# The first block's differential heads run together with the products of the other attention's queries, and both streams of heads begin at once

## The chip, the cores and the metric

One NeuronCore of a Trainium2 chip runs the whole network in one launch. The metric is the device time of one execution in microseconds (us). A core has TensorE (PE, the matrix engine, with a queue for weight loads, PEld), VectorE (DVE), ScalarE (ACT), GpSimd (POOL) and SyncE (SP, which issues most DMAs). Each engine works through a queue of its own in order and waits at semaphores for the others. Matmuls write to PSUM, which has eight banks of 128 x 512 floats.

## What is computed

Two layers over 256 context tokens and 256 latent tokens of width 1024. Each layer has a token mixer of three kinds of heads behind one input projection (`w_in`) and one output projection (`w_out`), and then a channel mixer: a SwiGLU block in the first layer, eight experts of which each token uses two in the second. All modulation (scales, shifts, gates) comes from products of a conditioning vector with `ada_w`. The two attentions, which matter here:

```
swa : 8 window heads of 64   softmax(q k^T / 8, with a sink) v      band of keys plus all context
diff: 4 heads, two maps each w = softmax(q0 k0^T) - lam * softmax(q1 k1^T);  out = norm(w v)
lru : a gated linear recurrence in both directions, 256 channels
out = concat(lru, swa, diff) @ w_out
```

In layer 0 the queries of all four blocks of 128 tokens are needed (blocks 0 and 1 are context, 2 and 3 latent), in layer 1 those of the latent blocks alone.

## The kernel before

Every product is made in three matmuls of rounded parts (`mm3`, lines 105 to 109): a weight is split into a high and a low part by a cast on ScalarE and a subtraction on VectorE (L126, L127).

`mixer` is the function around the change. It makes, for one layer: the recurrence's inputs and its coroutines (`self.scans`, driven by `fill_lru`); the keys and values; the queries of the differential heads; at last, with the columns from 512 on, the queries of the window heads: for each block tb in `order` (2, 3, 0, 1 in layer 0; 2, 3 in layer 1) `token_major` makes 24 matmuls into a bank `acc`, `rope` (L530 to L532) turns the latent blocks, and `swa_q` splits the result (L131, L132), transposes it (L543) and casts it back (L545).

Then `streams` runs two streams of coroutines in rounds. Stream a holds `diff` for each block, stream b holds `swa`. A step of `diff` is one head map (a latent block; two of a context block): score matmul (L669), maximum (L595), scaling (L670), exponential (L674) and, for every second map, the combination (L680 to L682), the transposes of the weights (L581), their copy (L585) and the product with the values (L686) into the block's output bank. A step of `swa` does the same for a window head (L611 to L615, L623, L627, L634). Stream b starts when six rounds have gone by (`if j == 1 and n < 6: continue`). After every second round `fill(1)` emits one piece of other work from `self.todo`: in layer 0 the sixteen ada steps (a DMA of 1 MB into one of the two `raw` buffers at L253 and four matmuls into bank A at L255), in layer 1 eight ada steps and four small builds of columns and rows. What is left over is emitted after the streams by `fill(99)`.

After the streams `project` loads `w_out` through the same two `raw` buffers (L793, L796), splits it and multiplies.

PSUM banks by tag: acc 2, S 3 (scores), T 2 (transposes), A 1. The order in which the program emits an instruction is its priority; the framework that builds the program then orders each engine's queue by priority and by its own estimate of what will be ready, so that work emitted later can stand ahead of work that has to wait.

Of the kernel before, what the change touches and what calls it, by code (L numbers as in the profile page):

```python
# [24 lines left out]
P = 128  # L25
# [51 lines left out]
class Trunk:  # L77
# [246 lines left out]
            nc.vector.tensor_tensor(out=G, in0=G, in1=self.lng(*ln)[:, None, :].to_broadcast([P, 2, KD]), op=ALU.mult)  # L324
        return G, B

    def streams(self, a, b):

        rest, live, tails, n = [list(a), list(b)], [None, None], [], 0
        while any(live) or any(rest) or tails:  # L330
            tails = [g for g in tails if next(g, self) is not self]
            for j in range(2):
                if j == 1 and n < 6:
                    continue
                if live[j] is None and rest[j]:
                    live[j] = rest[j].pop(0)
                if live[j] and next(live[j]) == "tail":
                    tails.append(live[j])
                    live[j] = None
            n += 1  # L340
            if n % 2 == 0:
                self.fill(1)
# [85 lines left out]
                    part(s0, kh, cb)  # L428
                    yield bs

    def token_major(self, uh, ul, ws, tb, c1=512):

        b = self.bank("acc")
        s = slice(tb * P, (tb + 1) * P)
        for k in range(KD):
            self.mm3(b[:, 0:c1], uh[k][:, s], ul[k][:, s], ws[k][0][:, 0:c1], ws[k][1][:, 0:c1], k == 0, k == KD - 1)
        return b
# [218 lines left out]
    def diff(self, l, tb, q, kT, V, mix, mp):  # L656
# [11 lines left out]
        for h0 in range(0, 8, G):  # L668
# [7 lines left out]
            if len(Ps) == 2:  # L676
# [6 lines left out]
                t = self.weights_t(p0, nk)  # L683
# [8 lines left out]
        sq = self.rp.tile([P, 512], F32, name="ra", tag="ra")[:, 0:256]  # L692
# [19 lines left out]
        b = self.bank("T")  # L712
        for k in range(2):
            nc.tensor.transpose(b[:, k * P:(k + 1) * P], m[:, k * P:(k + 1) * P], self.eye)
        hi, lo = (t[:, :, tb * P:(tb + 1) * P] for t in mp)
        self.split2(hi, lo, b[:, 0:256].rearrange("p (k t) -> p k t", k=2))


    def mixer(self, l, uh, ul, qtb, bd, products, prepare=None):
        nc, i, tc = self.nc, self.i, self.tc  # L720
        lat = qtb[0] == 2
        order = qtb if lat else [2, 3, 0, 1]
        view = lambda c0: self.w_in(l, c0)
        t0 = 256 if lat else 0
        with tc.tile_pool(name="pp", bufs=4) as self.pp, tc.tile_pool(name="kv", bufs=1) as kp, tc.tile_pool(name="st", bufs=2) as self.sp, \
                tc.tile_pool(name="qp", bufs=len(qtb)) as self.qp, tc.tile_pool(name="rp", bufs=1) as self.rp, \
                tc.tile_pool(name="sm", bufs=2) as self.sm, ExitStack() as es:
            y = kp.tile([P, 2, T - t0], F32, name="y")
            lru = es.enter_context(ExitStack())
            self.lp = lru.enter_context(tc.tile_pool(name="lru", bufs=1))  # L730
            xs, bs = [], [*products][-1]
            for cb in range(2):
                xs.append(self.lru_in(bs[cb]))
            for cb in range(2):
                self.lru_gate(cb, bs[2 + cb], t0, y)
            self.scans = [self.lru(l, cb, xs[cb], bd, y, t0) for cb in range(2)]
            kdT = kp.tile([P, 8, T], F32R, name="kdT")
            kT = kp.tile([P, 4, T], F32R, name="kT")
            dV = kp.tile([P, NTB, 256], F32, name="dV")
            V = kp.tile([P, NTB, P], F32, name="V")  # L740
            mix = {tb: kp.tile([P, 256], F32, name=f"mix{tb}") for tb in qtb}
            ws = self.chunk(view(1536))
            for tb in range(NTB):
                b = self.token_major(uh, ul, ws, tb)
                nc.scalar.copy(out=dV[:, tb], in_=b[:, 256:512])
                src = b[:, 0:256]
                self.keys(src if tb < 2 else self.rope(src, 8, 16, tb - 2, "32"), 8, 32, kdT, tb)
                self.fill_lru(1)
            ws = self.chunk(view(1024))
            dq = {}  # L750
            for tb in range(NTB):
                b = self.token_major(uh, ul, ws, tb, 512 if tb in qtb else 256)
                nc.scalar.copy(out=V[:, tb], in_=b[:, 128:256])
                src = b[:, 0:128]
                self.keys(src if tb < 2 else self.rope(src, 2, 32, tb - 2, "64"), 2, 64, kT, tb)
                if tb in qtb:
                    src = b[:, 256:512]
                    dq[tb] = self.diff_q(src if tb < 2 else self.rope(src, 8, 16, tb - 2, "32"))
                self.fill_lru(2)
            self.fill_lru(99)  # L760
            lru.close()
            if prepare:
                prepare()
            sqp = es.enter_context(tc.tile_pool(name="sq", bufs=len(qtb)))
            ws = self.chunk(view(512))
            sq = {}
            for tb in order:
                b = self.token_major(uh, ul, ws, tb)
                sq[tb] = self.swa_q(b if tb < 2 else self.rope(b, 8, 32, tb - 2, "64"), sqp)
            (hp, mh), (lp, ml) = self.pairs("mh"), self.pairs("ml")  # L770
            c0, c1 = qtb[0] * P, (qtb[-1] + 1) * P
            for cb in range(2):
                self.split2(mh[cb][:, c0:c1], ml[cb][:, c0:c1], y[:, cb])
            self.streams([self.diff(l, tb, dq[tb], kdT, dV, mix[tb], (hp[3], lp[3])) for tb in order],
                         [self.swa(l, tb, sq[tb], kT, V, (hp[1:3], lp[1:3])) for tb in order])
            self.fill(99)
        return mh, ml

# [641 lines left out]
```

## Time and profile before

| | |
|---|---|
| median of three runs | 1669.04 us (1667.8 to 1669.34) |
| the profiled execution | 1670.24 us, its span from first to last instruction 1668.5 us |
| TensorE busy | 1584.1 us, 95% of the span |
| VectorE busy | 1217.6 us, 73% |
| ScalarE busy | 919.0 us, 55% |
| mean granted TensorE clock | 0.976 of full speed |
| products of the window queries, layer 0 / layer 1 | about 131 to 157 us / 804 to 817 us |
| the streams, layer 0 / layer 1 | about 157 to 269 us / 817 to 893 us |

A busy time is the time in which an engine had an instruction under way; ends of matmuls are modelled, since they are pipelined, so a busy TensorE need not be at its best. A granted clock of 1.00 is 2.4 GHz, 0.50 is 1.2 GHz. In timelines the columns are start, duration, engine, line, operation, the tiles written and read, the shape and the count of merged instructions, and in brackets the idle time just before and what ended it.

### The profile page before, as it was taken

The page shows a single profiled execution, that of the slowest core. Times are in us where ns is not written, and L with a number is a line of the kernel's source. Part 1 is how long each engine was busy: PE and PEld are TensorE (multiplying, and loading weights), DVE is VectorE, ACT ScalarE, POOL GpSimd, SP SyncE. Part 2 cuts the span into 40 slices and gives each one's busy share as a digit, 9 for nine tenths or more (in the row PEclk, how much of TensorE's full clock was granted, in tenths as well). Part 3 has the DMA queues.
Part 4 walks back from the last instruction along what each step waited for, and adds up shares of the span by engine and source line. Part 5 has one row for each costly group of instructions (what it writes and reads, how often), then busy time and mean ns, then how long its engine had stood idle before and what let it go on. Part 6 is the DMA issues. An engine that isn't in the chain of part 4 may idle for free. (4 is left out here: it accounts for less than half of the span.)

```text
span 1668.5 us, 21566 instructions
## 1 busy us (share of the span) xinstructions
PE 1584.1 (95%) x7977; PEld 1227.8 (74%) x7977; DVE 1217.6 (73%) x1733; ACT 919.0 (55%) x1298; POOL 161.5 (10%) x131
## 2 busy tenths in 40 slices
PE   7999999999999999999899799999999999999995
PEld 3776566787777777777567588787887878878774
DVE  2678674654543335677976898999889898888987
ACT  2466565422222223246666487777676776767773
POOL 0000012250000000350002200101001010010101
PEclk8999999999999999999999799999999999999998
DMA  8313446334443336112347599898998989989890
GB/s 310 116 54 105 152 152 202 101 114 165 159 146 125 126 126 202 51 59 78 108 146 273 181 394 357 324 377 301 352 350 320 343 310 348 355 319 331 326 359 30
DMA packets 164584, 364.79 MB, mean 219 GB/s; under 512 B 8397, under 2 KB 46121, under 8 KB 159353
## 3 DMA queue, kind: packets, MB, share of 16 engines
q1 hardware_dynamic: 159472, 355.56, 60.6%
q0 software_dynamic: 1840, 6.67, 1.2%
q10 hardware_dynamic: 3160, 1.12, 0.3%
q8 instruction: 65, 1.06, 0.3%
q14 instruction: 47, 0.38, 0.1%
HBM read 362.27 MB, written 1.05 MB: 218 GB/s over the span
## 5 line engine op out<-in xcount | busy, mean ns | idle before, releaser
L127 DVE TENSOR_TENSOR wlo<-rawb,whi 128x1024 fp32r<-128x1024 f32 x362 | 436.0, 1249 | 34.4 <-ACT whi L126 30.7
L126 ACT CAST whi<-rawb 128x1024 fp32r<-128x1024 f32 x362 | 364.4, 1052 | 55.5 <-PE ps_h L109 31.7
L127 DVE TENSOR_TENSOR wlo<-raw,whi 128x1024 fp32r<-128x1024 f32 x214 | 268.8, 1281 | 45.2 <-ACT whi L126 43.9
L126 ACT CAST whi<-raw 128x1024 fp32r<-128x1024 f32 x214 | 217.9, 1051 | 145.2 <-DMA raw<-in_ffn_w_dram 52.0
L108 PE MATMUL ps_h<-wlo,th 128*128 128x512 f32 (+1 forms) x672 | 256.6, 382 | 14.3 <-DVE wlo L127 13.4
L107 PE MATMUL ps_h<-whi,th 128*128 128x512 f32 (+1 forms) x672 | 252.8, 376 | 0.0
L109 PE MATMUL ps_h<-whi,tl 128*128 128x512 f32 (+1 forms) x672 | 250.6, 373 | 0.0
L108 PEld LDWEIGHTS ps_h<-wlo,th 128*128 128x128 f32 x672 | 126.6, 188 | 52.0 <-DVE wlo L127 31.6
L107 PEld LDWEIGHTS ps_h<-whi,th 128*128 128x128 f32 x672 | 126.6, 188 | 22.5 <-ACT th L131 0.2
L109 PEld LDWEIGHTS ps_h<-whi,tl 128*128 128x128 f32 x672 | 126.7, 188 | 20.4 <-DVE tl L132 0.2
L108 PE MATMUL ps_Y<-wlo,gTh 128*128 128x512 f32 x308 | 122.4, 397 | 0.4
L109 PE MATMUL ps_Y<-whi,gTl 128*128 128x512 f32 x308 | 120.2, 390 | 0.0
L1160 POOL TENSOR_TENSOR hl<-hl,sct 128x512 f32<-128x512 f32 x26 | 45.0, 1758 | 677.4 <-DVE sct L1159 557.3
L107 PE MATMUL ps_Y<-whi,gTh 128*128 128x512 f32 x308 | 108.4, 390 | 0.0
L890 DVE TENSOR_TENSOR silu<-silu,ps_S 128x512 f32<-128x512 f32 x22 | 15.1, 686 | 114.6 <-PE ps_S L109 114.6
L107 PE MATMUL ps_acc<-uh,whi 128*128 128x512 f32 (+1 forms) x256 | 92.1, 365 | 2.3 <-ACT whi L126 2.3
L108 PE MATMUL ps_acc<-ul,whi 128*128 128x512 f32 (+1 forms) x256 | 94.0, 367 | 0.1
L109 PE MATMUL ps_acc<-uh,wlo 128*128 128x512 f32 (+1 forms) x256 | 92.0, 360 | 0.0
L108 PE MATMUL ps_S<-ul,whi 128*128 128x512 f32 (+1 forms) x240 | 85.7, 357 | 0.0
L107 PE MATMUL ps_S<-uh,whi 128*128 128x512 f32 (+1 forms) x240 | 85.6, 357 | 0.0
L109 PE MATMUL ps_S<-uh,wlo 128*128 128x512 f32 (+1 forms) x240 | 85.0, 355 | 0.0
L107 PE MATMUL ps_acc<-whi,uh 128*128 128x512 f32 (+1 forms) x176 | 71.0, 403 | 0.0
(352 smaller groups left out, 2881.4 us busy)
## 6 DMA issues: line engine op xcount, KB each, us to landing
rawb<-in_moe_w_dram SPq DMA_DIRECT2D x181, 1024.0 KB, 7.0
raw<-in_moe_w_dram SPq DMA_DIRECT2D x50, 1024.0 KB, 6.9
raw<-in_ada_w_dram SPq DMA_DIRECT2D x40, 1024.0 KB, 4.9
raw<-in_ffn_w_dram SPq DMA_DIRECT2D x33, 1024.0 KB, 5.6
raw<-in_w_in_dram SPq DMA_DIRECT2D x16, 1024.0 KB, 5.1
aw<-in_ada_w_dram SPq DMA_DIRECT2D x16, 512.0 KB, 6.7
raw<-in_w_out_dram SPq DMA_DIRECT2D x16, 512.0 KB, 5.9
lg<-in_ln_g_dram POOLq DMA_DIRECT2D x4, 512.0 KB, 4.1
```

The source lines that it names most:

```text
L107: mm(out, lhsT=ah, rhs=bh, start=start, stop=False)
L108: mm(out, lhsT=ah, rhs=bl, start=False, stop=False)
L109: mm(out, lhsT=al, rhs=bh, start=False, stop=stop)
L126: nc.scalar.copy(out=hi, in_=v)
L127: self.last = nc.vector.tensor_tensor(out=lo, in0=v, in1=hi, op=ALU.subtract)
L890: nc.vector.tensor_tensor(out=t, in0=t, in1=b3, op=ALU.mult)
L1160: (nc.vector if quick and nn else nc.gpsimd).tensor_tensor(out=hl[:, b, cs], in0=hl[:, b, cs], in1=t, op=ALU.add)
```

## The change

`streams` takes the first coroutine of stream a as it stands (`live`) and starts stream b in the first round. `mixer` creates the differential coroutines before the products of the window queries. After the first three blocks' products in layer 0 it advances the first of them by two steps each, after each of the two blocks in layer 1 by three: six steps in either layer. The products go to banks acc and A in turn, since the first coroutine takes one of the two acc banks for its output. The output tiles of `diff` are handed over by a function, as they are allocated only after the products.

```diff
-    def streams(self, a, b):
+    def streams(self, a, b, live):
 
-        rest, live, tails, n = [list(a), list(b)], [None, None], [], 0
+        rest, live, tails, n = [list(a), list(b)], [live, None], [], 0
         while any(live) or any(rest) or tails:
             tails = [g for g in tails if next(g, self) is not self]
             for j in range(2):
-                if j == 1 and n < 6:
-                    continue
                 if live[j] is None and rest[j]:
...
-    def token_major(self, uh, ul, ws, tb, c1=512):
+    def token_major(self, uh, ul, ws, tb, c1=512, bank="acc"):
 
-        b = self.bank("acc")
+        b = self.bank(bank)
...
-        hi, lo = (t[:, :, tb * P:(tb + 1) * P] for t in mp)
+        hi, lo = (t[:, :, tb * P:(tb + 1) * P] for t in mp())
...
-            for tb in order:
-                b = self.token_major(uh, ul, ws, tb)
+            out = []
+            parts = [self.diff(l, tb, dq[tb], kdT, dV, mix[tb], lambda: out) for tb in order]
+            for j, tb in enumerate(order):
+                b = self.token_major(uh, ul, ws, tb, bank=("acc", "A")[j % 2])
                 sq[tb] = self.swa_q(b if tb < 2 else self.rope(b, 8, 32, tb - 2, "64"), sqp)
+                if j < 3:
+                    for _ in range(3 if lat else 2):
+                        next(parts[0])
             (hp, mh), (lp, ml) = self.pairs("mh"), self.pairs("ml")
+            out += [hp[3], lp[3]]
...
-            self.streams([self.diff(l, tb, dq[tb], kdT, dV, mix[tb], (hp[3], lp[3])) for tb in order],
-                         [self.swa(l, tb, sq[tb], kT, V, (hp[1:3], lp[1:3])) for tb in order])
+            self.streams(parts[1:], [self.swa(l, tb, sq[tb], kT, V, (hp[1:3], lp[1:3])) for tb in order], parts[0])
             self.fill(99)
```

## Rows read from the trace of the kernel before

**Rows 1.** The page, busy time of each engine (share of the span), instructions.

```profile
PE 1584.1 (95%) x7977; PEld 1227.8 (74%) x7977; DVE 1217.6 (73%) x1733; ACT 919.0 (55%) x1298; POOL 161.5 (10%) x131
```

**Rows 2.** Table by stage, layer 0: stretch, its length, busy us by engine, PEclk, DMA.

```profile
130.00:157.00 27.00, 26.93 (x137) 21.91 (x136) 24.18 (x42) 15.24 (x25) 0.61 (x1) 1.00 0.13 44
157.00:166.40 9.40, 8.48 (x43) 2.52 (x41) 7.56 (x20) 6.72 (x15) 0.00 (x0) 1.00 0.66 223
```

**Rows 3.** The same table, layer 1 (engines: PE, PEld, DVE, ACT, POOL).

```profile
810.70:817.40 6.70, 6.70 (x36) 5.39 (x34) 6.67 (x12) 5.33 (x8) 0.00 (x0) 1.00 0.01 2
817.40:837.50 20.10, 14.00 (x71) 6.65 (x69) 16.57 (x40) 10.47 (x24) 0.00 (x0) 0.83 0.52 185
837.50:866.00 28.50, 27.96 (x200) 17.80 (x199) 19.61 (x53) 17.92 (x46) 2.38 (x3) 1.00 0.37 129
```

**Rows 4.** Timeline of TensorE where layer 1's streams begin.

```profile
815.94 1.06 PE L543 MATMUL ps_T<-cst,st 128*128 128x128 f32 x8
...
819.03 1.04 PE L255 MATMUL ps_A<-raw,sc 128*2 128x512 f32 x8
823.53 1.02 PE L255 MATMUL ps_A<-raw,sc 128*2 128x512 f32 x2 [3.46 <-DMA raw<-in_ada_w_dram]
826.20 1.97 PE L543 MATMUL ps_T<-cst,st 128*128 128x128 f32 x8 [1.65 <-ACT qT L545]
827.82 1.63 PE L669 MATMUL ps_S<-kdT,qT 128*128 128x512 f32 x3
829.25 1.05 PE L581 MATMUL ps_T<-cst,p 128*128 128x128 f32 x4
830.23 1.64 PE L255 MATMUL ps_A<-raw,sc 128*2 128x512 f32 x8
...
835.83 0.63 PE L581 MATMUL ps_T<-cst,p 128*128 128x128 f32 x4 [0.72 <-DVE nb L670]
```

**Rows 5.** Timeline of VectorE in the same place.

```profile
812.00 0.67 DVE L545 CAST qT<-ps_T 128x512 fp32r<-128x512 f32 x1
...
818.48 0.68 DVE L531 TENSOR_TENSOR rb<-ps_acc,cst 128x512 f32<-128x512 f32 x1
...
828.41 0.68 DVE L545 CAST qT<-ps_T 128x512 fp32r<-128x512 f32 x1
```

**Rows 6.** VectorE's groups by form, 156.7 to 269 us: count, busy us, mean ns.

```profile
L595 DVE TENSOR_REDUCE mx<-ps_S 128x1 f32<-128x512 f32 x32 | 21.7, 686 | 10.6 <-PE ps_S L669 6.1 <-PE ps_S L615 4.4
...
L682 DVE SCALAR_TENSOR_TENSOR p<-p,ls 128x512 f32<-128x512 f32 x8 | 6.0, 746 | 0.1
...
L681 DVE TENSOR_SCALAR ls<-ls,nlam 128x1 f32<-128x1 f32 x16 | 4.3, 269 | 0.2
...
L670 DVE TENSOR_SCALAR nb<-mx 128x1 f32<-128x1 f32 x16 | 2.3, 147 | 0.1
```

**Rows 7.** Table by stage for the ada matmuls alone (bank A), layer 0's streams.

```profile
156.70:269.00 112.30, 29.83 (x128) 2.74 (x128) 2.77 (x4) 2.28 (x4) 1.00 0.46 151
```

**Rows 8.** Timeline of SyncE's DMA issues, end of layer 0's streams.

```profile
251.07 0.89 SPq L793 DMA_DIRECT2D raw<-in_w_out_dram  x2
260.74 1.38 SPq L796 DMA_DIRECT2D raw<-in_w_out_dram  x2
```

**Rows 9.** Timeline of TensorE, end of layer 0's streams.

```profile
259.66 1.03 PE L255 MATMUL ps_A<-raw,sc 128*2 128x512 f32 x6
...
264.92 0.55 PE L581 MATMUL ps_T<-cst,p 128*128 128x128 f32 x3
265.82 0.50 PE L107 MATMUL ps_acc<-whi,mh 128*128 128x512 f32 x1 [0.36 <-ACT whi L126]
```

**Rows 10.** DMA issues, 120 to 275 us: count, KB each, median us to landing.

```profile
raw<-in_w_out_dram SPq DMA_DIRECT2D x8, 512.0 KB, 4.8
```

**Rows 11.** The page's groups: the cast of a weight tile (busy us, mean ns).

```profile
L126 ACT CAST whi<-raw 128x1024 fp32r<-128x1024 f32 x214 | 217.9, 1051 | 145.2 <-DMA raw<-in_ffn_w_dram 52.0
```

## The prediction

> **What bounds the kernel now.** I read the engine totals first. TensorE is busy for 1584 of 1668.5 us and VectorE for 1218 [rows 1], so work that is only moved about can win no more than the places where TensorE stands still. Then I read the stage table around the two attention stages, one for each layer. In layer 0 the products before the streams (130 to 157 us) leave TensorE 0.07 us idle out of 27, and the first 9.4 us of the streams, where only the differential heads run, leave 0.92 [rows 2]. Layer 0 has almost nothing to give. In layer 1 the same place reads otherwise: from 817.4 to 837.5 TensorE is busy for 14.00 of 20.10 us at a mean granted clock of 0.83, while VectorE is busy for 16.57 [rows 3]. TensorE's timeline shows the hole itself [rows 4]: 3.46 us before an ada matmul that waits for its DMA, 1.65 us before the transposes of the second block's queries, 0.72 us before the first exponentials' next transposes. What follows the hole runs at the lower of the two clock levels, 1.2 GHz (the same forms take up to twice as long).
>
> Why is nothing else there for TensorE? Only differential heads have been emitted (the window heads come in at the seventh round), and VectorE is behind: the rope of block 3 reads its bank at 818.48 and the last cast of its transposed queries is at 828.41 [rows 5], because the gated recurrence, the rope and the maxima of the heads share a queue that is busy for 6.67 of 6.70 us beforehand [rows 3].
>
> **What the change does, part by part.** Six head steps of the first differential block leave the streams and stand behind the blocks' products (two after each of the first three blocks in layer 0, three after each of the two in layer 1). Both streams then begin in the first round. No computation is added or removed, only a bank changes: every second block's product goes to bank A, since the block's output now holds one of the two acc banks during the products.
>
> Layer 1, upper bound. The idle time is 3.46 + 1.65 + 0.72 = 5.83 us. The slower clock costs, by rows of the same form at both levels: eight transposes 1.97 against 1.06, four transposes 1.05 against 0.63, one ada step 1.64 against 1.04 [rows 4], together 1.93; three score matmuls of 1.63 us at the same ratio add 0.7. All of it is 8.4 us, if window heads, whose first block's queries had their last cast at 812.00 [rows 5], fill the hole.
>
> Layer 1, lower bounds. VectorE has 20.10 - 16.57 = 3.53 us free in this stretch. If all its work there must still come first, the gain is 3.5. Below zero: the first three heads now ask VectorE for work in the 6.7 us beside block 3's products, where it has 0.03 us free. A head costs it a maximum (0.686) and a scaling (0.147), a pair of heads another 0.269 + 0.746 [rows 6]: three heads with one pair are 3.5 us. If TensorE's queue waits for all of that, the gain turns into a loss of 3.5. I take the upper half, about 6, because the work that is pushed back (rope and transposes of block 3) is needed only by the second window block, eight rounds later, and VectorE has 28.50 - 19.61 = 8.9 us free in the next 28.5 [rows 3]. From this I take off 1 us: two ada steps of 1.04 us fill TensorE just before the hole now (the second at 819.03 [rows 4]), and they will have to wait, since bank A is held until block 3's rope has read it (818.48 at the earliest). Layer 1: -5.0.
>
> Layer 0, first the idle time: -0.9 of the 0.92 us. The heads' VectorE work, 6 x 0.833 + 3 x 1.015 = 8.0 us, meets 27.00 - 24.18 = 2.82 us of free time [rows 2, 6]; the 5.2 that don't fit move into the first rounds, where VectorE has been idle for 1.84 of 9.4, or TensorE waits for them. I put that at nothing in the forecast, as products are at hand all along to cover a wait, and at 5.2 in a rival.
>
> Layer 0, the ada steps. A step is emitted after every second round. Before: 6 + 24 + 2 = 32 rounds, 16 steps, none left. After: 26 rounds, 13 steps; the last three are emitted behind the streams. Two things follow. The matmuls of these steps cover 29.83 us [rows 7] where 16 unbroken steps of 1.04 would take 16.6; the 13.2 above that are steps which other work breaks into two or three pieces. Three steps that run unbroken save 3 x 13.2 / 16 = 2.5 at most, at least nothing; I take 1. Against this stands the output projection: its weights use the same two buffers. Before, its two pairs of loads go out at 251.07 and 260.74 [rows 8], the second right behind the last ada matmuls at 259.66, and its first product runs at 265.82 [rows 9]. A later last step delays them. If the projection is not held up this costs nothing; if the three steps only run after the last head, about 7.6 (the second rival has the working). Now the last step too is emitted behind every head, and still it ran before the last transposes of weights (259.66 against 264.92), so steps do run ahead of their place, and I take a quarter: +1.9. Layer 0 together: -0.9 - 1.0 + 1.9 = 0.
>
> In layer 1 the rounds fall from 24 to 18 and the fillings from 12 to 9; what is left over are small column and row builds, and the eight ada steps still lie inside the streams. I count nothing. POOL's queue gets the first block's norm earlier, SP's order is the same, and the stages behind both places are filled by TensorE or wait in a chain for it, so a gain passes through to the end.
>
> Sum: -5.0 + 0 = -5.0 us. The profiled execution took 1670.24 (a span of 1668.5 and 1.74 around it), which gives 1665.2. The median of the runs, 1669.04, is 1.2 lower; against it the forecast is **1664.0**.
>
> **Where a page speaks against it.** At 823.53 TensorE does nothing for 3.46 us while one matmul waits for a DMA, though eight transposes, emitted earlier, stand behind it [rows 4]. The Trainium skill, "TensorE: Matmul & The Clock Gate", Part 2, says that matmuls stay in program order and only weight loads are pulled ahead. By that rule an early head whose exponential is late holds up every product behind it; the trace agrees so far as the queue did stand still, and can't show whether the transposes were ready (they waited another 1.65 us for ScalarE afterwards). What it would do here is the third rival.
>
> **The rivals.** (1) *The hole only moves.* VectorE's backlog is the true limit, and TensorE waits for maxima instead of transposes. For it: 6.67 of 6.70 us busy before the hole [rows 3]. Against: VectorE itself idles 3.5 us within it. Gain 1 to 2 us in all, 1667.5.
> (2) *The last ada steps hold the projection.* Let E be the end of layer 0's streams and steps 14 to 16 run only then. Steps 14 and 15 take 1.04 each, so the projection's first load goes out at E + 2, lands 4.8 later [rows 10], and after a cast of 1.05 [rows 11] the first product comes at about E + 8. Step 16 fills 1 us of these 6, so 5 are idle, and behind them 2.6 may be lost at the lower clock as after the hole in layer 1: 7.6 in place of the 1.9. Layer 0 is then +5.7, layer 1 stays at -5.0: +0.7, 1669.7, no difference. For it is the count of rounds, against it that steps run ahead of their place.
> (3) *Heads block the products, and the kernel is slower.* The place is TensorE's queue beside the blocks' products; the price is VectorE's 5.2 us in layer 0, and 3.5 in layer 1, where the gain falls to 1.5. The other terms of layer 0 cancel, so this is 5.2 - 1.5 = +3.7, 1672.7. It ends slower than before once more than 5.0 of these 8.7 us are waited for. For it is a VectorE without free time beside the products; against it that products stand ready to be put ahead of each transpose.
> (4) *More than forecast.* All 8.4 of layer 1, 0.9 of layer 0, 2.5 of unbroken steps, no delay: 11.8, 1657.2.
>
> **How the numbers follow.** Forecast 0.50, with a range of its own from 1660.5 to 1667; rival 1 0.18, rival 2 0.12, rival 3 0.12, rival 4 0.08. A difference of 0.2% (3.3 us) is about what a measurement of this kernel tells from none. Below 1665.7 lie 0.44 of the forecast, rival 4 and 0.02 of rival 1: faster 0.54. Above 1672.4 lie rival 3 and 0.03 of rival 2 (where layer 1 gives only its 3.5): slower 0.15. The rest, 0.31, is no difference. The range runs from 1658, which leaves out most of rival 4, to 1672.5, which leaves out most of rival 3.
>
> **What would show it.** In the trace after: score matmuls, exponentials and transposes of the first differential block among the products; in layer 1 the 20 us behind the products with at most 2 to 3 us of TensorE idle and the clock at its upper level throughout; block 3's rope later than 818. The stretch from the end of the products to the projection shorter by about 5 us in layer 1 and about the same in layer 0, counted from the last product of the queries less the heads' own work. I am wrong if layer 0's projection starts with TensorE waiting for w_out (rival 2), if TensorE shows waits for p or nb between products (rival 3), or if the hole of layer 1 stands at another place with the same size (rival 1).

## The result and the profile after

The change makes the kernel slower. The median is 1689.06 us (four runs, 1685.76 to 1691.61) against 1668.74 us (1667.8 to 1669.34), a ratio of 1.0118 with a 95% interval from 1.0104 to 1.0133. The profiled span is 1689.4 us where it was 1668.5.

The page's engine totals come first (to be read beside [rows 1]).

```profile
PE 1589.8 (94%) x7977; PEld 1231.0 (73%) x7977; DVE 1216.4 (72%) x1733; ACT 918.4 (54%) x1298; POOL 162.5 (10%) x131
```

The counts of instructions are the same on every engine, and TensorE is busy for 5.7 us more. The span is 20.9 us longer, so 15 of them are new idle time. To find the place I took the starts of the same instructions in both traces and split the span at them.

| stretch | before | after | difference |
|---|---|---|---|
| start to the first rope of the window queries in layer 0 | 137.10 | 135.16 | -1.9 |
| from there to the same rope in layer 1 (**L0**) | 673.16 | 689.47 | +16.3 |
| from there to the router's first work on TensorE (**L1**) | 105.12 | 110.83 | +5.7 |
| from there to the end | 753.12 | 753.94 | +0.8 |

Both places of the change lost, layer 0 three times as much as layer 1. L0 and L1 are used as names of these stretches from here on.

**Layer 0.** The table by stage shows it in three steps: products of the queries, streams, output projection. First the kernel before, cut at its own stage ends (columns as in [rows 2]).

```profile
128.00:156.60 28.60, 28.53 (x144) 22.71 (x143) 26.05 (x48) 17.25 (x28) 0.96 (x1) 1.00 0.16 47
156.60:267.60 111.00, 108.73 (x729) 62.05 (x727) 74.73 (x216) 70.03 (x198) 9.94 (x13) 1.00 0.47 152
267.60:315.00 47.40, 47.40 (x229) 38.85 (x229) 24.07 (x49) 15.59 (x20) 14.69 (x13) 1.00 0.44 133
```

The same for the changed kernel; the third line is the 2.4 us in which the last two ada steps run behind the last head.

```profile
128.00:162.60 34.60, 31.91 (x159) 25.53 (x158) 29.69 (x62) 20.62 (x38) 0.67 (x1) 0.95 0.10 34
162.60:263.40 100.80, 98.53 (x691) 59.03 (x689) 66.15 (x194) 61.06 (x181) 9.95 (x13) 1.00 0.42 145
263.40:265.80 2.40, 2.33 (x19) 0.35 (x18) 0.89 (x2) 1.22 (x3) 1.65 (x2) 1.00 0.66 195
265.80:329.00 63.20, 52.64 (x229) 42.02 (x226) 26.26 (x50) 17.40 (x21) 13.05 (x11) 0.89 0.54 129
```

The products took 0.07 us of idle time before and take 2.7 now; the streams idle for 2.27 us in either kernel; the projection, without any idle time before, now stands still for 10.6 us and runs at a mean granted clock of 0.89. The timeline of SyncE's issues shows why (to be read beside [rows 8]).

```profile
263.51 2.19 SPq L796 DMA_DIRECT2D raw<-in_w_out_dram  x3
265.92 2.26 SPq L799 DMA_DIRECT2D raw<-in_w_out_dram  x2
268.23 0.60 SPq L796 DMA_DIRECT2D raw<-in_w_out_dram  x1
268.88 5.65 SPq L799 DMA_DIRECT2D raw<-in_w_out_dram  x2
```

GpSimd issues the token rows, 2 MB, in the same microseconds:

```profile
264.05 0.92 POOL L1325 DMA_DIRECT2D hc<-in_ctx_dram  x1 [10.19 <-PE ps_T L647]
264.97 0.73 POOL L1326 DMA_DIRECT2D hl<-in_x_dram  x1
```

In the kernel before they went out after the first half of `w_out` (251.07 and 260.74 [rows 8]):

```profile
268.28 0.92 POOL L1322 DMA_DIRECT2D hc<-in_ctx_dram  x1 [9.15 <-PE ps_T L649]
```

So 4 MB of `w_out` and 2 MB of rows move at once, and the median load of `w_out` takes 20.6 us to land where it took 4.8 [rows 10]:

```profile
raw<-in_w_out_dram SPq DMA_DIRECT2D x8, 512.0 KB, 20.6
```

TensorE's timeline shows the cost (to be read beside [rows 9]). The last two ada steps, sixteen records in the trace (eight for a step), begin at 263.71, behind the last head; the first product of the projection runs at 276.07, and two more waits follow.

```profile
276.07 0.80 PE L107 MATMUL ps_acc<-whi,mh 128*128 128x512 f32 x1 [4.48 <-ACT whi L126]
...
281.80 0.74 PE L107 MATMUL ps_acc<-whi,mh 128*128 128x512 f32 x2 [1.59 <-ACT whi L126]
...
288.44 0.73 PE L107 MATMUL ps_acc<-whi,mh 128*128 128x512 f32 x2 [1.69 <-ACT whi L126]
```

The casts that TensorE waits for wait themselves for the DMA:

```profile
274.97 1.04 ACT L126 CAST whi<-raw 128x1024 fp32r<-128x1024 f32 x1 [7.87 <-DMA raw<-in_w_out_dram]
280.70 1.04 ACT L126 CAST whi<-raw 128x1024 fp32r<-128x1024 f32 x1 [3.57 <-DMA raw<-in_w_out_dram]
```

**Layer 1.** TensorE's waits in the 112 us from 824 to 936, grouped by the releaser (total us, times, longest).

```profile
PE ps_S L667 <- ACT p L672: 2.8, 1, 2.8
PE ps_T L712 <- POOL mix L707: 2.3, 1, 2.3
PE ps_S L609 <- ACT p L625: 1.0, 1, 1.0
PE ps_S L609 <- ACT p L672: 0.8, 1, 0.8
PE ps_h L1204 <- DVE res L816: 0.8, 1, 0.8
PE ps_A L255 <- DMA raw<-in_ada_w_dram: 0.7, 1, 0.7
```

The 3.46 us before an ada matmul and the 1.65 us before the queries' transposes [rows 4] are gone. A wait of 2.8 us has come in their place, and one of 2.3 us on GpSimd that the kernel before does not have. These waits alone do not make the loss. Over L1 the tables by stage add up to this, the kernel before first:

```profile
sum 105.10, PE 97.01 PEld 67.90 DVE 77.88 ACT 65.42 POOL 9.95; mean PE 19.40 PEld 13.58 DVE 15.58 ACT 13.08 POOL 1.99
sum 110.90, PE 101.98 PEld 69.16 DVE 78.20 ACT 65.67 POOL 9.89; mean PE 20.40 PEld 13.83 DVE 15.64 ACT 13.13 POOL 1.98
```

TensorE idles for 8.1 us before and 8.9 after; the other 5.0 us are longer busy time for the same work, at a mean granted clock of 0.95 in place of 0.97 and with the ada steps broken into more pieces (they cover 14.3 us of TensorE's time in L1 where they covered 11.8).

The wait of 2.8 us is read from three engines. TensorE:

```profile
832.14 0.40 PE L109 MATMUL ps_A<-whi,ul 128*128 128x512 f32 x1
835.38 0.49 PE L667 MATMUL ps_S<-kdT,qT 128*128 128x512 f32 x1 [2.84 <-ACT p L672]
835.80 1.87 PE L255 MATMUL ps_A<-raw,sc 128*2 128x512 f32 x2
```

ScalarE in the same place:

```profile
831.31 1.28 ACT L501 ACT_TABLE_LOAD   x1 [1.47 <-DVE nb L668]
832.61 0.63 ACT L501 ACTIVATE H<-H 128x512 f32<-128x512 f32 x1
833.25 1.28 ACT L672 ACT_TABLE_LOAD   x1
834.55 0.69 ACT L672 ACTIVATE p<-ps_S,nb 128x512 f32<-128x512 f32 x1
```

VectorE (to be read beside [rows 5]):

```profile
833.74 0.68 DVE L528 TENSOR_TENSOR ra<-ps_A,cst 128x512 f32<-128x512 f32 x1
...
834.93 0.68 DVE L529 TENSOR_TENSOR rb<-ps_A,cst 128x512 f32<-128x512 f32 x1
```

Three early heads had filled the three score banks. Their exponentials come behind the recurrence's own function on ScalarE (L501), with a table load of 1.28 us ahead of each; the first exponential ends at 835.2, and only then is a score bank free. VectorE is part of it: ScalarE's first table load had itself waited 1.47 us for L668, and VectorE is busy for all of the 14 us from 828 to 842. The ada steps could not stand in, since bank A is let go by the rope at 834.93 + 0.68 = 835.61. TensorE had a free bank for neither a score nor an ada step. What follows runs at the lower clock level (the granted clock is 0.50 from 836 to 838; the two merged records of an ada step take 1.87 us, where two such take 1.02 at 1.00 [rows 4]).

At the streams' end the projection's first product comes later. It runs at 903.55, 9.6 us ahead of the last transposes of the streams (913.18); before it ran 16.2 us ahead of them (877.64 and 893.80), in the gaps of the last heads. It stands behind the transposes that wait 2.33 us for GpSimd:

```profile
900.44 0.58 PE L712 MATMUL ps_T<-cst,mix 128*128 128x128 f32 x2 [2.33 <-POOL mix L707]
903.55 0.67 PE L107 MATMUL ps_acc<-whi,mh 128*128 128x512 f32 x1
```

### The profile page after: what moved, and what is told of

Its sections match the earlier page's. It is cut to its first block, busy times and chain, and to the rows that moved or that the text cites. A ratio compares the mean times of both kernels' runs of the same rounds, so it can differ in the third digit from the quotient of the medians.

```text
span 1689.4 us, 21550 instructions
## 1 busy us (share of the span) xinstructions
PE 1589.8 (94%) x7977; PEld 1231.0 (73%) x7977; DVE 1216.4 (72%) x1733; ACT 918.4 (54%) x1298; POOL 162.5 (10%) x131
## 5 line engine op out<-in xcount | busy, mean ns | idle before, releaser
L108 PE MATMUL ps_h<-wlo,th 128*128 128x512 f32 (+1 forms) x672 | 257.2, 383 | 14.2 <-DVE wlo L127 13.2
L893 DVE TENSOR_TENSOR silu<-silu,ps_S 128x512 f32<-128x512 f32 x22 | 15.1, 686 | 116.2 <-PE ps_S L109 116.2
L131 ACT CAST gh<-silu 128x512 fp32r<-128x512 f32 x22 | 13.6, 619 | 101.6 <-DVE silu L893 101.6
```

The source lines that it names most:

```text
L108: mm(out, lhsT=ah, rhs=bl, start=False, stop=False)
L131: self.copied = self.nc.scalar.copy(out=hi, in_=src)
L893: nc.vector.tensor_tensor(out=t, in0=t, in1=b3, op=ALU.mult)
```

## The experiments

All times are medians. The kernel before had 1670.33 us in the session of the first four kernels, 1669.14 in that of the next four, 1668.36 in the third, 1669.79 with the last one. The last two columns are the differences of the stretches L0 and L1 from the kernel before, from one profiled execution of each kernel. That execution can lie off the median (the change: 1691.15 us, heads_alone: 1684.9, before_dense: 1676.1), and a stretch that a kernel doesn't touch differs by up to 1.0 us (L0 of layer1_fills).

| kernel | us (lowest to highest) | ratio to before (95%) | L0 | L1 |
|---|---|---|---|---|
| the change | 1689.06 (1685.76 to 1691.61) | 1.0118 (1.0104 to 1.0133) | +16.3 | +5.7 |
| layer0_alone | 1683.52 (1680.58 to 1684.97) | 1.0073 (1.0054 to 1.0092) | +16.1 | 0.0 |
| layer1_alone | 1674.39 (1672.39 to 1676.73) | 1.0028 (1.0018 to 1.0038) | -0.5 | +4.9 |
| at_once_alone | 1678.53 (1674.76 to 1682.61) | 1.0057 (1.0038 to 1.0075) | +1.8 | +4.4 |
| fills_back | 1676.88 (1675.97 to 1678.07) | 1.0039 (1.0025 to 1.0053) | +4.9 | -0.5 |
| late_fills_l0 | 1678.68 (1676.29 to 1680.14) | 1.0052 (1.0035 to 1.0069) | +3.3 | +4.6 |
| heads_alone | 1680.55 (1678.97 to 1684.9) | 1.0065 (1.0048 to 1.0082) | +13.5 | +1.5 |
| at_once_l1_fills | 1677.04 (1674.29 to 1680.06) | 1.0044 (1.0028 to 1.006) | -0.5 | +7.4 |
| before_dense | 1678.55 (1676.1 to 1679.78) | 1.0058 (1.0042 to 1.0075) | +5.7 | +3.6 |
| half_crowd | 1686.95 (1683.89 to 1688.18) | 1.0098 (1.008 to 1.0115) | +12.6 | +5.9 |
| layer1_fills | 1670.33 (1667.99 to 1672.4) | 1.0006 (0.9997 to 1.0016) | +1.0 | +0.8 |
| both_mended | 1674.34 (1673.31 to 1676.65) | 1.0032 (1.0022 to 1.0042) | +3.4 | +0.8 |
| ada_between | 1675.35 (1674.24 to 1679.88) | 1.0039 (1.0027 to 1.0051) | -0.4 | +5.4 |
| rows_behind | 1681.96 (1676.77 to 1683.36) | 1.0065 (1.0045 to 1.0085) | +6.5 | +5.5 |

In the diffs `lat` is true in layer 1.

### Which layer, which half of the change

**layer0_alone** and **layer1_alone** keep the change in one layer. The early steps, the start of stream b and the alternating banks are as before in the other.

```diff
# layer0_alone; in layer1_alone (0, 3)[lat] and (6, 0)[lat]
-                    for _ in range(3 if lat else 2):
+                    for _ in range((2, 0)[lat]):
...
+                if j == 1 and n < (0, 6)[lat]:
+                    continue
```

> The change in layer 0 alone; layer 1 as before. By the shift of the same instructions between the two traces (14.4 us from the start to the products of layer 1's last queries), both theories expect +14 to +16, 1683 to 1685. If layer 1's shift of another 5.7 us only follows from layer 0, +20.

> The change in layer 1 alone; layer 0 as before. From the shifts between the traces (14.4 us before layer 1's products of queries, 20.1 at the first product of the experts' routing): +5 to +6, 1673.5 to 1675. The prediction's working for this layer said -5, 1664.

Measured: 1683.52 and 1674.39 us. Both lie in their ranges. The losses about add up, +16.1 in L0 and +4.9 in L1 against +16.3 and +5.7 with both (in the medians 13.2 and 4.1 of 20.3), so the two layers are treated as two separate cases.

**at_once_alone** lets both streams begin at once, has no early heads and keeps the products in bank acc; **heads_alone** has the early heads and the six rounds before stream b.

```diff
# at_once_alone
-                    for _ in range(3 if lat else 2):
+                    for _ in range((0, 0)[lat]):
# heads_alone
+                if j == 1 and n < (6, 6)[lat]:
+                    continue
```

> Both streams begin in the first round, but no head stands among the products and all products go to acc: the second half of the change alone. It has the same 13 and 9 fillings as the changed kernel. If the count of fillings alone makes the loss, layer 0 loses 14 us or more: 1683 and up. Theory A goes by where the last ada step stands: here 55 instructions ahead of the last head's transposes, more than before the change (29), so layer 0 loses nothing, 1664 to 1672.

> The second half of the change alone: the first block's differential heads run with the query products in both layers, while the sliding heads wait six rounds as before. No ada step is left behind the last head of layer 0 in the queue. Crowd theory: no crowd at w_out, landing about 5 us in layer 0. What the heads cost among the products (6 to 7.5 us later end of the products) comes back only if the streams are shorter by as much; with six rounds of differential heads alone they are about as long as before, so the streams' end in layer 0 is 4 to 8 us later than before and layer 1 about the same: 1678 to 1684 us. Rival (heads among the products are free and only the start at once hurts): 1664 to 1670 us.

Measured: 1678.53 and 1680.55 us. Neither half gains. at_once_alone has the same 13 fillings in layer 0 as the change and loses little there; its last ada step runs at 253.02, far ahead of the last head, so the count of pieces left over does not make the loss of layer 0 by itself. Its time is above the 1664 to 1672 us of theory A, mostly because of layer 1: the streams there are 3.1 us shorter, but the projection begins 13.5 us later (11.5 counted from the start of L1) and L1 ends at +4.4. The reason is read from ScalarE: the projection's first product needs an `acc` bank, and the differential stream's last output lets go of it by a copy. In the kernel before this copy comes at 875.17, as this stream ends six rounds ahead of the other:

```profile
875.17 0.37 ACT L696 COPY ro<-ps_acc 128x256 f32<-128x256 f32 x1
```

With both streams from the start they end together, the copy is 14 us later (12 counted from the start of L1), and the first product, at 877.64 before, follows at 891.17:

```profile
889.52 0.37 ACT L694 COPY ro<-ps_acc 128x256 f32<-128x256 f32 x1 [1.18 <-PE ps_acc L684]
```

heads_alone falls in the range written down for the cost of the heads, but one part of that expectation missed: `w_out` lands in 10.1 us, not 5. Its last ada step in layer 0 runs at 273.01, only 1.6 us ahead of the last transposes, so that `w_out` (270.64, 274.10) again meets the token rows (275.28).

### The fillings, taken back

**fills_back** is the change with a filling after rounds 1, 3 and 5 as well, in both layers. **late_fills_l0** adds three in layer 0 alone, in rounds 9, 11 and 13: the early part of the streams is that of the changed kernel, only the last steps come ahead of the last head. **layer1_fills** is layer1_alone with the fillings of rounds 1, 3 and 5. **both_mended** is the change with late_fills_l0 in layer 0 and rounds 1, 3 and 5 in layer 1.

```diff
-            if n % 2 == 0:
+            if n % 2 == 0 or n in ((9, 11, 13), (1, 3, 5))[lat]:     # both_mended
                 self.fill(1)
```

> The changed kernel with three more fillings, in the first, third and fifth round of the streams, so that 16 ada steps of layer 0 and 12 pieces of layer 1 lie inside the rounds as before the change. Theory A (the last two ada steps stand behind the last head in TensorE's queue and hold both raw buffers, so that all loads of w_out go out at once with the token loads): the last ada step now stands 18 TensorE instructions ahead of the last head's transposes, so most of the 18 us that the projection of layer 0 loses goes away: 1671 to 1677. Theory B (the heads among the products cost the time, through VectorE): nothing changes, 1687 to 1691.

> The changed kernel with three further fillings in layer 0's streams (rounds 9, 11 and 13), layer 1 as in the changed kernel. The early heads and the two streams that begin at once stay; the one thing that differs is that the last two ada steps stand ahead of the last head of layer 0 again. Crowd theory (these two steps hold both raw buffers, so that all 4 MB of w_out and the 2 MB of token rows move together): the w_out landing in layer 0 falls from 20.6 us to 5 to 7 us, the first w_out product comes 5 to 7 us earlier than in the changed kernel, PE's clock in the products is 1.00 again and the time is about 1679 to 1681 us (8 to 10 us under the changed kernel). Rival (the heads among the products and the waits on their banks are the loss): the products still end 6 us late, the streams still end where they end now, and the time stays within 2 us of the changed kernel's 1689.

> The change in layer 1 alone (early heads and both streams at once), with three further fillings there in rounds 1, 3 and 5; layer 0 as before. Theory of the left-over pieces: the change in layer 1 without these fillings cost 4 to 6 us, all of it because the small pieces left over and the first w_out products no longer fill the end of the streams; with them layer 1 gains 0 to 1 us, since the heads among the products lengthen those by 1 us and shorten the streams by 2 to 3: 1667 to 1669.5 us. Rival (the cost lies in the heads and the hole, which are the same as in the change): 1672 to 1675 us.

> The whole change with the fillings put back in both layers: rounds 9, 11 and 13 in layer 0, rounds 1, 3 and 5 in layer 1. If the two causes add up (10.5 us of w_out's crowd in layer 0, 5 to 6 us of left-over pieces in layer 1), what stays is what the early heads cost in layer 0, 3 to 5 us: 1671 to 1674 us. If they don't add up (the time saved in layer 0 is lost again behind it), 1676 to 1680 us as with the fillings of layer 0 alone.

Measured: 1676.88, 1678.68, 1670.33 and 1674.34 us.

fills_back lies in the range of its theory A, late_fills_l0 0.3 us under its own. late_fills_l0 settles the trigger in layer 0: L0 falls from +16.3 to +3.3 and the time by 10.4 us. Its DMA issues from 240 to 330 us:

```profile
raw<-in_w_out_dram SPq DMA_DIRECT2D x8, 512.0 KB, 4.9
```

SyncE issues them at 261.35 and 263.71 again, ahead of the token rows (270.51):

```profile
261.35 0.89 SPq L796 DMA_DIRECT2D raw<-in_w_out_dram  x2
263.71 1.39 SPq L799 DMA_DIRECT2D raw<-in_w_out_dram  x2
```

layer1_fills settles layer 1: L1 falls from +4.9 to +0.8, and the median of 1670.33 is not told from the kernel before (0.9997 to 1.0016). That is nearer to the theory of the left-over pieces, though 0.8 us over its range. The early hole is still there, of the same size, but the later waits on GpSimd and on the DMA are gone (TensorE's waits from 810 to 917, the largest three):

```profile
PE ps_S L669 <- ACT p L674: 2.8, 1, 2.8
PE ps_h L1206 <- DVE res L818: 0.8, 1, 0.8
PE ps_T L581 <- ACT p L627: 0.7, 1, 0.7
```

What came back is idle time, and what the layer might have gained went into busy time. The tables by stage over L1, layer1_alone first:

```profile
sum 110.00, PE 100.64 PEld 67.67 DVE 77.94 ACT 65.56 POOL 9.86; mean PE 20.13 PEld 13.54 DVE 15.59 ACT 13.11 POOL 1.97
sum 105.90, PE 100.09 PEld 66.36 DVE 77.37 ACT 65.75 POOL 9.64; mean PE 20.02 PEld 13.27 DVE 15.47 ACT 13.15 POOL 1.93
```

TensorE's idle time in L1 goes from 8.1 us before to 9.4 in layer1_alone and 5.8 in layer1_fills, so with the fillings the change does win 2.3 us of it. But TensorE is busy for 3.1 us more than before, and the ada steps, broken more often, cover 16.7 us where they covered 11.8 (layer1_alone: 14.1). fills_back has the same layer 1 and -0.5 there, in an execution whose granted clock stays at 1.00 in L1, so the 0.8 is not told from nothing.

both_mended shows that the two causes add up: L0 +3.4, L1 +0.8, a time 0.3 us over the range for that case and well under the 1676 to 1680 us of the other. What stays in layer 0 is read from its table by stage, cut as above:

```profile
128.00:164.00 36.00, 32.64 (x166) 25.36 (x165) 31.62 (x67) 22.59 (x42) 0.96 (x1) 1.00 0.12 37
164.00:268.70 104.70, 103.33 (x698) 59.08 (x696) 67.30 (x196) 62.83 (x184) 9.95 (x13) 1.00 0.47 158
268.70:317.50 48.80, 48.63 (x237) 39.55 (x237) 25.54 (x50) 16.93 (x21) 14.70 (x13) 1.00 0.47 138
```

TensorE's busy time over the three is that of before (184.60 against 184.66 us). Its idle time is 4.9 us where it was 2.3, and the products' stage alone has 3.4 of it. It is two waits of the queue among the products:

```profile
146.99 0.47 PE L107 MATMUL ps_A<-whi,uh 128*128 128x512 f32 x1 [2.57 <-DVE rb L529]
...
153.93 0.66 PE L579 MATMUL ps_T<-cst,p 128*128 128x128 f32 x4 [0.76 <-ACT qT L543]
```

The first is the fourth block's product (the changed kernel has the same wait of 2.57 us at 145.02). It needs bank A, which the second block's product holds until its rope has read it, and the rope stands in VectorE's queue with the early heads and the recurrence. The third block's product, whose `acc` bank the first block's rope had read by 140.12, stands behind it, at 156.90; why the order puts it there was not tried, and no run keeps the heads there without these waits.

### Controls on the pace of fillings

**before_dense** is the kernel before with a filling after every round. **at_once_l1_fills** has layer 0 as before and in layer 1 both streams at once, no early heads and three further fillings. **ada_between** is the kernel before, in which layer 1 fills in one ada step behind each block's product.

```diff
# before_dense
-            if n % 2 == 0:
+            if n % (1, 1)[lat] == 0:
# at_once_l1_fills
+                if j == 1 and n < (6, 0)[lat]:
...
+            if n % 2 == 0 or n in ((), (1, 3, 5))[lat]:
# ada_between, in mixer's loop over the blocks
+                if lat:
+                    self.fill(1)
```

> The kernel before with one change: the streams fill in a piece after every round instead of every second one, in both layers. A control on the fillings, with nothing of the change. The ada steps end some 40 us earlier and in fewer broken pieces, w_out's loads and whatever else is left come earlier, and the heads at the end of the streams have no filler. Theory that the pace of fillings is what costs the changed kernel its time, whatever the heads do: too few and too early fillings both cost, here 3 to 8 us, as PE idles and slows at the end of the streams: 1672 to 1677 us. Rival (only fillings that come too late cost): within 2 us of 1668.7, or faster.

> Layer 0 as before. In layer 1 the two streams begin at once, with no early heads, and three further fillings (rounds 1, 3 and 5) so that as many pieces are filled in as before. With both streams from the start but without these fillings, layer 1's streams had ended 3 us earlier after their start and the output projection lost 7.5 us to pieces left over. Theory of the left-over pieces: with the fillings restored the projection begins and ends as before, and 1 to 3 us of gain are left: 1665.5 to 1669 us against 1668.7. Rival (the projection is late because the streams' end takes away the gaps that its products used to fill): the gain of the streams is lost again whatever is filled: 1670 to 1675 us.

> The kernel before, in which layer 1 also fills in one ada step behind each of the two blocks of query products; nothing of the change. TensorE's hole at the start of layer 1's streams has 3.46 us of idle time before an ada matmul whose DMA could only go out when an earlier step had let go of its buffer. Theory that the hole is a matter of what is at hand for TensorE: with two steps emitted earlier the next two loads go out earlier, the wait on the DMA falls from 3.46 to 0 to 1 us, and the time is 1665.5 to 1668 us. Rival (VectorE's backlog sets the pace, and a filled hole only moves the steps): the time stays within 1.5 us of 1668.7.

Measured: 1678.55, 1677.04 and 1675.35 us, all above every range written down. More filling is no better than less: before_dense, which has nothing of the change, loses 5.7 us in L0 and 3.6 in L1. at_once_l1_fills shows that the fillings alone don't mend layer 1: beside at_once_alone, from which only they tell it apart there, its ada steps cover 13.9 us in place of 11.8 and TensorE is busy for 98.1 us in place of 95.8; its bank is let go at 892.25 and the first product of the projection comes at 892.99, 15.4 us later than before. Both are wanted there, no pieces left over and an `acc` bank free six rounds early; of the versions with both streams at once, only those with the early heads and the fillings have both (fills_back, layer1_fills, both_mended). ada_between was meant to fill the hole of layer 1 from the other side. The wait on the DMA fell from 3.46 only to 2.83, one step further on, so the hole is not filled by emitting two steps earlier. Of the 5.4 us that L1 lost, 1.0 is idle time and 4.4 busy time; the ada steps cover 15.1 us in place of 11.8.

### What the crowd at the projection consists of

**half_crowd** is the change without the two extra buffers of the projection in layer 0, so that the second half of `w_out` can't be loaded at once. **rows_behind** is the change with the token rows issued by SyncE, behind the loads of the first half of `w_out`.

```diff
# half_crowd
-                    self.project(0, mh, ml, all4, gate, h, lambda tb: self.norm(h(tb)), raw2)
+                    self.project(0, mh, ml, all4, gate, h, lambda tb: self.norm(h(tb)))
# rows_behind, in project behind the loads and splits of a half
+            if n == 0 and rows:
+                with self.tc.issue_after(d.ins):
+                    rows()
```

> The changed kernel, in which layer 0's output projection loads its second half of w_out through the two raw buffers too, not through two buffers of its own: so 2 MB of w_out at the most are under way beside the 2 MB of token rows, where the changed kernel has 4 MB. The two ada steps still stand behind the last head. Theory of the crowd (the delay of the first w_out product comes from transfers that share the DMA engines): the first w_out product in layer 0 comes 3 to 6 us earlier than in the changed kernel (276.1), though the second half of the weights comes later; the time is 1681 to 1687 us. Rival (the delay comes from the raw buffers that the two ada steps hold, and what moves beside it doesn't matter): the first product stays within 1 us of 276 and the time is 1689 to 1694 us, as the second half waits for the first one's casts.

> The changed kernel, in which layer 0's 2 MB of token rows (hc, hl) are issued by SyncE behind the loads of the first half of w_out, not by GpSimd at the streams' end. The two ada steps still stand behind the last head, the buffers are as in the changed kernel. Theory of the shared transfers: the first pair of w_out lands within 5 to 7 us in place of 11, the first w_out product in layer 0 comes at 270 to 272 us in place of 276.1, and the time is 1683 to 1687 us, as the rest of w_out still moves beside the rows. Rival (the first product waits for w_out's own first half, whatever moves beside it, because its loads go out late): the first product stays at 275 to 277 us and the time is 1688 to 1692 us.

Measured: 1686.95 and 1681.96 us. The first product comes at 276.71 and 274.85 us. Counted from the end of the last ada matmuls it comes after 5.1 us before, 10.2 in the changed kernel, 10.7 in half_crowd and 7.3 in rows_behind: the first case goes with the rival, the second lies between the two theories, so about half of this delay goes away when the rows wait. The time goes with the shared transfers: 2.1 us less without the second half, 7.1 us less (under the range) when the rows wait. From the last ada step to the last product of the projection it is 65.1 us in the changed kernel, 62.5 in half_crowd and 55.7 in rows_behind; before it was 54.9. Once it has begun, the projection of rows_behind runs without a break, where the changed kernel has 54 records and 13.79 us of busy time in the same 16 us:

```profile
284.00:300.00 16.00, 16.00 (x72) 13.28 (x71) 8.44 (x11) 3.39 (x5) 3.87 (x3) 1.00 0.92 215
```

So of the 10.1 us that the stretch behind the last ada step lost, 9.4 go away when the token rows wait. rows_behind changes the rows' queue along with their order (SyncE's in place of GpSimd's), and the two are not told apart. These differences are of one profiled execution each: the one of the changed kernel lies 2.1 us above its median, which is most of the difference between 9.4 in the stretch and 7.1 in the time.

No version here is faster than the kernel before; the nearest, layer1_fills, is level with it.

## Why the prediction was wrong

The forecast was 1664.0 us and the range ended at 1672.5; the change takes 1689.06. The sum was -5.0; the measured stretches give +16.3 and +5.7.

**What bounds the kernel** held. Layer 0 had almost no idle time to win: its streams idle for 2.27 us before and after, and of the 0.92 us in their first 9.4 us, which the forecast counted as won, 0.57 stay. Layer 1 had the hole.

**Layer 1, the hole (-6).** Partly right, then blocked. The wait on the DMA and the one on the queries' transposes went, and in layer1_alone the 19.4 us behind the products are busy for 15.67 us, where the kernel before has 14.00 in 20.1. But the bound "window heads fill the hole" left out what a head needs besides its queries: a score bank, and an exponential on ScalarE. The working counted VectorE's 6.70 us and said nothing of ScalarE's queue, where the recurrence's last function and two table loads of 1.28 us stand ahead of the first exponential. Rival 1 (the hole only moves) describes what is seen, a wait of 2.84 us, half the old idle time; it named VectorE as the reason, and what ends the wait is the first exponential on ScalarE, which frees a score bank. VectorE is behind it as well, since ScalarE had waited 1.47 us for it and it also frees bank A.

**Layer 1, "I count nothing" for the left-over fillings.** This is the step that failed in layer 1. The count, nine fillings in place of twelve, stood in the text; the judgment that small column and row builds cost nothing was an opinion without a row. Putting the three fillings back takes L1 from +4.9 to +0.8, so this term is 4.1 us, 3.6 of it idle time. What they cost is shown by the projection's first product, 8.3 us later in layer1_alone than before (10.2 counted from the start of L1): the left-over pieces are emitted ahead of the projection, whose products had filled the gaps of the last heads. Why the order places it behind the GpSimd wait there was not tried. Even with the fillings the forecast of -5.0 is missed by 5.8 us: only 2.3 us of idle time are won, and TensorE's longer busy time, 3.1 us, has no term in the sum.

**Layer 0, `w_out` (+1.9).** This step failed twice. The chance, a quarter, was taken from the one last step that had run ahead of its place; two of the three left-over steps ran behind the last head. And the price of 7.6 us assumed the landing of 4.8 us [rows 10] for loads that go out later: the first product was to come about 8 us behind the streams' end, and it comes 12.7 behind it (276.07 and 263.4). Steps ahead of the head (late_fills_l0) bring 13.0 us of the stretch back and 10.4 of the time. The missing part is that the token rows go out at the streams' end whatever the ada steps do. Before, the first half of `w_out` was ahead of them by 17.2 and 7.5 us; after, it met them. The prediction looked at the queue that the loads stand in and not at what else starts on the same event. Rival 2 had the mechanism right, with a chance of 0.12; its price of 7.6 us was 13.0 in the stretch.

**Layer 0, the heads among the products (nothing in the forecast, 5.2 in rival 3).** The waits exist: 2.57 and 0.76 us, together 3.3 where 5.2 was the price. Rival 3 had the place right, TensorE's queue beside the products, though the waits are for the rope (rb) and a cast of the queries (qT), not for p or nb, the sign that the prediction gave. The argument for nothing, that products are at hand to cover a wait, fails by the change's own bank: the product that stands next in the queue is the one that waits for bank A. The prediction listed "only a bank changes" and used it for the ada steps alone.

**Layer 0, unbroken ada steps (-1.0).** Not measured in layer 0. In the changed kernel the steps cover 26.60 us where they covered 29.83 [rows 7], but the stages around them run at a lower clock, so the busy time can't show the gain. both_mended has the same busy time as the kernel before (184.60 and 184.66 us), with its steps broken almost as often (28.81 us). Layer 1 speaks for the term, and against the change: two records of a step by themselves take 1.02 us and all eight 1.04, and in layer1_fills the steps cover 4.9 us more than before while TensorE is busy for 3.1 us more. That the pieces make this busy time is argued from such pairs; no run changes the breaks alone. The prediction used the cost of a broken step for layer 0 and not for layer 1, where the change breaks more of them.

**The range** left out the rivals' joint case. Rivals 2 and 3 (the latter in layer 0, at 3.3 us) and the lost gain of layer 1 came true together, and nothing in the profile made them exclude each other; each was priced as if the others stayed away.

**Of the page cited,** the Trainium skill, "TensorE: Matmul & The Clock Gate", Part 2: matmuls stay in program order. The trace after agrees where products wait (the whole queue stands for 2.57 us behind one product). In layer 1 it can't be told, as the ada step behind the waiting score had no bank before 835.61 either.

## What to carry to other kernels

When a change shortens a loop that also hands out other work, count the pieces that are left over and follow each to the buffer it holds and to who loads next through that buffer; then list what else starts on the same event, since a transfer that was early and cheap becomes expensive when it meets the others. Filler handed out too early is missing at the end of such a loop (before_dense lost 5.7 and 3.6 us), and a stage that follows can itself be that filler: a stream that ends early frees the bank for it. Count busy time beside idle time: layer1_fills won 2.3 us of the one and lost 3.1 of the other. Moving work into a stage where TensorE has no idle time cost 3.3 us of waits here.

## What was not expected of the hardware

The 16 DMA engines were busy throughout the crowd, but moved less than just before it. The table by stage of the changed kernel has a DMA share of 1.08 and 0.97 from 276 to 284 and from 284 to 300 us, at 176 and 211 GB/s, against 371 GB/s at a share of 1.01 right before:

```profile
270.00:276.00 6.00, 1.59 (x8) 1.19 (x6) 0.04 (x1) 1.03 (x1) 0.33 (x1) 0.50 1.01 371
276.00:284.00 8.00, 6.05 (x21) 4.43 (x22) 2.62 (x4) 3.13 (x6) 0.00 (x0) 0.79 1.08 176
284.00:300.00 16.00, 13.79 (x54) 10.63 (x53) 6.17 (x7) 2.94 (x3) 2.56 (x2) 0.89 0.97 211
```

So the same share went with rates that differ by a factor of two, and a full share doesn't say that the bytes come as fast as they can. What set this rate was not tried.

The same wait of 2.57 us among the products left the granted clock at 1.00 in both_mended and is followed by a stage mean of 0.95 in the changed kernel.

The table load on ScalarE costs 1.28 us and no more here: the exponential starts 0.02 us behind it. The Trainium skill, "ScalarE: Activation LUTs", "What ACT_TABLE_LOAD costs", gives about 1283 ns and a drain of some 1380 ns on top; the first figure agrees, the drain doesn't show (the load at 833.25 begins as the function before it ends at 833.24).
